# New costs in the emission clock of a two-layer diffusion block: TensorE, ScalarE and the port that VectorE shares with GpSimd

## The chip, the cores and the metric

The kernel runs on one core of a Trainium2 chip. A core has five engines with an instruction queue each: TensorE (matmuls, in the profile PE, with its weight loads as PEld), VectorE (DVE), ScalarE (ACT), GpSimd (POOL) and SyncE (SP, which here only issues transfers). Each works through its own queue in the order in which the program put instructions there, and they wait for one another by semaphores. The metric is the device time of one execution in microseconds (us); lower is better.

## The reference

Two layers work on 512 latent tokens and 256 context tokens of width 1024, in float32. A layer is

```
h += 0.5*gate * swiglu(modulate(rmsnorm(h)), w_gu, w_down)   # FFN 1, hidden width 2816
h += gate * (concat(retention, fourier, attention, gmlp)(modulate(rmsnorm(h)) @ w_in) @ w_out)
h += 0.5*gate * swiglu(modulate(rmsnorm(h)), w_gu, w_down)   # FFN 2
```

Shift, scale and gate come from `silu(cond) @ ada_w + ada_b`, nine vectors of 1024 for each layer, one set for the latent tokens and one for the context. Retention runs in both directions with a decay per head, the Fourier part is a two-dimensional transform, attention has four query and two key heads with normalized and rotated keys, and gMLP gates by a mix over chunks of 128 tokens. The context is not carried past the mixing of the last layer. At the end stands an RMS norm of the latent tokens.

## The kernel before, in words

**Arithmetic.** The activations stand transposed in SBUF (tile `H`: features on partitions, 768 tokens along the free side). Every weight block of 128x512 is read from HBM into a `raw` tile and split into a high and a low part (`w`): ScalarE casts the high part to fp32r, and VectorE or GpSimd subtracts it from the block to give the low part. The moving side is split in the same way, and a product is three matmuls (`mm3`: high·high, high·low, low·high; L241 and L243). Most FFN blocks are multiplied by Strassen's scheme in Winograd's form, seven products where eight would stand, whose sums and differences of blocks are made on GpSimd (weights, `w_sums`, written back into `raw`) and on VectorE or GpSimd (activations, `t_task` and `hid_sums`).

**Order.** Nothing is scheduled by a compiler: the program is written out by Python generators ("tasks") that are run by a small event loop (`run`, L179). Each task yields a time, or a condition, at which it wants to go on. The loop has one clock, `k.t`, which is the modelled end of the last matmul put out, and picks the task of the highest priority whose time is not later than `k.t`. If there is none, the clock is moved on. So the modelled cost of an instruction decides nothing on the chip by itself; it decides which instruction is put next into each engine's queue, and for some operations into whose queue.

The model is small. Each matmul adds to the clock in `pe` (L228). Each of VectorE (`V`), ScalarE (`A`) and GpSimd (`G`) has a clock of its own, moved in `Eng.__call__` (L126) by a fixed cost, plus the free size over a rate, plus a cost for each operand of one element. `Times` keeps, for each 64 columns of each tile, when it is written and read, and a hop of 110 ns between engines.

**Where the modelled clocks decide.** Four places matter here.

- `w_copies` (L429) puts out the next weight cast when `A.t <= k.t + slack`, `w_subs` (L441) the next weight subtraction when `V.t <= k.t + slack`, with a slack of 1500 ns for the two blocks that TensorE needs next, of 600 for the two after them and of 200 beyond; or at once where TensorE's task already asks for the block (`force`). A block that lies three or more ahead goes to GpSimd if `G.t <= k.t < V.t`.
- `any2` (L218) gives a subtraction, sum or product of two SBUF operands to the engine that would end it first: `max(V.t, k.t) + 68 + n/0.96` against `max(G.t, k.t) + 100 + n/0.42`.
- `norm_task` (L963) gives the addition of the shift to VectorE or to ScalarE by a comparison of the same kind (L995), and goes on to the next feature block when `V.t <= k.t + 1000`.
- Everything else yields the modelled time at which its operand is ready (`at`, `rdy`).

In an FFN stage the work on TensorE is one task (`ffn`: `pair`, seven products of 24 matmuls for each pair of hidden blocks; `down_fast` and `down`, the second matrix), so its order is given, and only the batches of the modulation product (`ada`, eight matmuls of 256 columns by `mmq`, L254) are put between. In a mixing stage some ten tasks share TensorE. `hid_task` (L1103) makes SiLU times the second half and splits it, `hid_sums` (L1272) the sums for `down_fast` (L1317), `t_task` (L1065) those for `pair`. `upd` (L1425) adds a finished PSUM bank to `H` on VectorE.

Of the kernel before, what the change touches and what calls it, by code (L numbers as in the profile page):

```python
# [39 lines left out]
def _free(ap):  # L40
    n = 1
    for x in ap.shape[1:]:
        n *= x
    return n
# [8 lines left out]
class Times:  # L53


    def __init__(self):
        self.tiles = {}
        self.rings = {}
        self.live = set()
        self.last = {}  # L60
        self.seq = 0
# [57 lines left out]
class Eng:  # L119
# [6 lines left out]
    def __call__(self, name, *args, cost=None, **kw):  # L126
        getattr(self.eng, name)(*args, **kw)  # L127
        aps = [x for x in list(args) + list(kw.values()) if hasattr(x, "tensor")]
        out = aps[0]
        n = max(_free(x) for x in aps)  # L130
        if cost is None:
            cost = self.fixed + n / self.rate + self.ptr * sum(1 for x in aps if _free(x) == 1)
        if name == "activation" and args[2] in TABLES and args[2] != self.table:
            self.table = args[2]
            cost += 1283.0
        writes = [out] + ([kw["accum_out"]] if "accum_out" in kw else [])
        self.t = self.k.T.op(self.num, self.t, cost, aps[1:], writes)
        return self.t + HOP


class Kernel:
    FAR, SB, NS = 3, 130.0, 3
    RP = 2
    NM, NK = 3, 0
    HV, SL = 4, 1500.0
# [4 lines left out]
    def __init__(self, tc, I, out, pools):  # L150
        self.tc, self.nc, self.I, self.out = tc, tc.nc, I, out
        self.pools = pools
        self.t = 0.0
        self.tick, self.cols, self.cold = 0, 0.0, True
        self.T = Times()
        self.V = Eng(self, tc.nc.vector, 1, 68.0, 0.96, 60.0)
        self.A = Eng(self, tc.nc.scalar, 2, 88.0, 1.2, 93.0)
        self.G = Eng(self, tc.nc.gpsimd, 3, 100.0, 0.42, 0.0)
        self.dt = 0.0
        self.tasks = []  # L160
        self.flags = set()
        self.mcols = [16, 0]
        self.mod0 = self.rawlim = 0
        self.ulive = 0
        self.nready = {}
        self.ps = pools["ps"].tile([P, 4096], F32, tag="b", name="b", bufs=1)
        self.psn = self.T.psn = self.ps.tensor.name
        self.free = set(range(8))
        self.T.add(self.ps, 4096, 0.0)
        self.nacc = {}  # L170
        self.nrs = {}
        self.hcnt = {}
# [55 lines left out]
    def pe(self, cols, rows, floor, reads, out):  # L228

        start = self.T.op(0, self.t, 0.0, reads, [out])  # L230
        k = int(start // TICK)
        if k != self.tick:
            self.cold = k > self.tick + 1 or self.cols < 3060.0
            self.tick, self.cols = k, 0.0
        cost = max(cols / 1.2 if self.cold else 2.5 + cols / 2.4, floor)
        self.cols += cols * rows / 128.0
        self.t = self.T.op(0, start, cost, reads, [out])

# [11 lines left out]
    def mmq(self, out, k, x, start, stop):  # L250


        q = 32 * (k % 4)
        self.nc.tensor.matmul(out[q:q + 32], self.cs[:, k], x, start=start, stop=stop)  # L254
        self.pe(2 * _free(x), 128, 60.0, [self.cs[:, k], x], out)

    def mm3(self, out, a, b, start, stop, more=False):
        self.mm(out, a[0], b[0], start, False, more)
# [1302 lines left out]
    def ret_core(self, l, p):  # L1561
# [27 lines left out]
        for i in range(2):  # L1589
# [4 lines left out]
            for q0, nq, keys in parts:  # L1594
                po = None
                pend = []
                for ki in range(len(keys) + 2):
                    if ki < len(keys):
# [11 lines left out]
                        yield  # L1610
                    if len(pend) > self.RP or ki >= len(keys) and pend:
                        kj, kt, t, ok = pend.pop(0)
# [639 lines left out]
```

## Time and profile before

| | |
|---|---|
| time, median of 3 runs | 2707.93 us (2704.53 to 2708.25) |
| profiled execution: its time | 2709.11 us |
| profiled execution: its span, first to last instruction | 2707.0 us |
| busy TensorE / VectorE / GpSimd / ScalarE | 96% / 74% / 50% / 47% |
| mean granted TensorE clock | 0.99 |
| matmul records | 17308 |

The span is 2.1 us less than the execution's own time. An engine's busy share is an average over stages; for TensorE the ends of matmuls are modelled by the profile, so 96% doesn't mean that it works at its peak in all that time. A time in ns behind a count in a row is the mean of one instruction; where an instruction waits for a port in the middle of its work, that wait is in its time.

### The profile page before, as it was taken

The numbers are of one execution on the slowest core, as the hardware profiler recorded it, in microseconds if no ns is written. First come the engines' busy times: TensorE is split into PE (matmuls) and PEld (weight loads), VectorE is DVE, ScalarE is ACT, GpSimd is POOL, SyncE is SP. The second block draws the span as 40 slices with busy tenths as digits, with TensorE's granted clock in tenths as the row PEclk, the third lists the DMA queues.
The fourth block names the chain that finished last, engine by engine and source line by source line (L and its number), as shares of the span: only waits on it lengthen the run. The fifth ranks groups of instructions, "written<-read, shape, count | busy, mean of one in ns | idle before, by whom it ended". The sixth has DMA issues, their size and how long they took to land.

```text
span 2707.0 us, 45375 instructions
## 1 busy us (share of the span) xinstructions
PE 2611.7 (96%) x17308; PEld 2442.5 (90%) x17308; DVE 2014.0 (74%) x3473; ACT 1269.3 (47%) x2620; POOL 1345.2 (50%) x1094
## 2 busy tenths in 40 slices
PE   7999999999999999999999989999999999999998
PEld 5888999998797988888999989999999797999998
DVE  5765787877578785656887877878878677877776
ACT  5433444455645554343444534444446545544445
POOL 3535666733222253546765547668734231654443
PEclk9999999999999999999999999999999999999999
DMA  8456222121111145553123111221232111122332
GB/s 289 138 167 210 71 70 87 63 81 55 51 44 47 40 144 191 172 187 109 63 63 102 55 47 63 64 93 63 63 104 63 51 60 42 48 94 94 105 99 78
DMA packets 242778, 252.62 MB, mean 93 GB/s; under 512 B 12188, under 2 KB 226432, under 8 KB 242560
## 3 DMA queue, kind: packets, MB, share of 16 engines
q1 hardware_dynamic: 236304, 246.82, 28.5%
q10 hardware_dynamic: 6256, 2.90, 0.4%
q8 instruction: 136, 2.23, 0.3%
q14 instruction: 82, 0.67, 0.1%
HBM read 247.59 MB, written 2.10 MB: 92 GB/s over the span
## 4 chain that ended last, share of the span: by engine, by line
PE 72%; DVE 18%; issue 3%; ACT 2%; DMA 2%; POOL 2%; SPq 0%; ACTq 0%; DVEq 0%; POOLq 0%
PE b L241 41%; PE b L243 28%; DVE u L127 7%; DVE w L127 6%; DVE t L127 3%; PE b L254 2%; PE b L282 2%; DVE H L127 2%; DMA raw<-in_ffn_w_gu_dram 1%; ACT w L127 1%; DMA u<-in_ada_w_dram 1%; ACT u L127 1%; ACT t L127 1%; POOL u L127 0%; POOL raw L127 0%
## 5 line engine op out<-in xcount | busy, mean ns | idle before, releaser
L241 PE MATMUL b<-u,w 128*128 128x384 f32 (+1 forms) x8736 | 1465.3, 326 | 30.7 <-DVE u L127 21.4
L241 PEld LDWEIGHTS b<-u,w 128*128 128x128 f32 x8736 | 1424.0, 189 | 61.0 <-DVE u L127 28.9
L127 ACT CAST w<-raw 128x512 fp32r<-128x512 f32 x949 | 578.9, 621 | 626.9 <-PE b L241 255.2
L127 DVE TENSOR_TENSOR w<-raw,w 128x512 fp32r<-128x512 f32 x688 | 663.0, 972 | 231.4 <-ACT w L127 219.6
L127 POOL TENSOR_TENSOR raw<-raw 128x512 f32<-128x512 f32 x416 | 616.9, 1504 | 397.2 <-DMA raw<-in_ffn_w_gu_dram 138.1
L127 POOL TENSOR_TENSOR w<-raw,w 128x512 fp32r<-128x512 f32 x261 | 371.0, 1433 | 543.6 <-ACT w L127 495.2
L243 PE MATMUL b<-u,w 128*128 128x256 f32 (+2 forms) x3888 | 590.9, 309 | 17.7 <-ACT u L127 5.8
L243 PEld LDWEIGHTS b<-u,w 128*128 128x128 f32 x3888 | 543.0, 194 | 44.8 <-issue 10.2
L127 DVE SCALAR_TENSOR_TENSOR H<-b,modG,H 128x128 f32<-128x128 f32 (+3 forms) x832 | 368.5, 474 | 154.1 <-PE b L243 85.4
L243 PE MATMUL b<-w,u 128*128 128x256 f32 x2172 | 286.6, 288 | 1.8 <-DVE w L127 1.8
L243 PEld LDWEIGHTS b<-w,u 128*128 128x128 f32 x2172 | 270.0, 192 | 12.0 <-issue 6.8
L127 ACT COPY t<-b 128x384 f32<-128x384 f32 (+5 forms) x287 | 123.5, 431 | 209.6 <-PE b L241 98.1
L127 ACT CAST u<-u 128x384 fp32r<-128x384 f32 (+4 forms) x318 | 140.8, 464 | 121.1 <-DVE u L127 103.1
L127 DVE TENSOR_TENSOR u<-u 128x384 fp32r<-128x384 f32 (+8 forms) x227 | 183.0, 819 | 12.9 <-ACT u L127 12.1
L127 POOL TENSOR_TENSOR u<-u 128x384 fp32r<-128x384 f32 (+2 forms) x137 | 123.0, 907 | 93.2 <-ACT u L127 92.5
L243 PE MATMUL b<-u 128*64 128x256 f32 (+7 forms) x516 | 141.1, 371 | 0.0
L127 DVE TENSOR_TENSOR t<-t,b 128x384 f32<-128x384 f32 (+3 forms) x216 | 106.2, 494 | 43.3 <-PE b L241 42.3
L127 POOL TENSOR_TENSOR nacc<-nacc,t 128x256 f32<-128x256 f32 (+2 forms) x112 | 89.7, 802 | 95.6 <-ACT t L127 91.6
L127 ACT CAST u<-t 128x384 fp32r<-128x384 f32 (+2 forms) x162 | 74.1, 471 | 114.1 <-DVE t L127 107.3
L243 PEld LDWEIGHTS b<-u 128*128 128x128 f32 (+2 forms) x516 | 81.6, 176 | 47.0 <-issue 34.4
L127 ACT CAST u<-b 64x256 fp32r<-64x256 f32 (+3 forms) x175 | 77.9, 454 | 75.3 <-PE b L282 72.7
L127 POOL TENSOR_TENSOR rs<-mse,mhalf 128x2 f32<-128x2 f32 (+4 forms) x41 | 45.1, 1104 | 115.4 <-DVE mse L127 106.1
(95 smaller groups left out, 1660.7 us busy)
## 6 DMA issues: line engine op xcount, KB each, us to landing
raw<-in_ffn_w_gu_dram SPq DMA_DIRECT2D x176, 512.0 KB
adaraw<-in_ada_w_dram SPq DMA_DIRECT2D x113, 512.0 KB
raw<-in_ffn_w_down_dram SPq DMA_DIRECT2D x88, 512.0 KB
raw<-in_w_in_dram SPq DMA_DIRECT2D x28, 512.0 KB
raw<-in_w_out_dram SPq DMA_DIRECT2D x32, 256.0 KB
u<-in_ada_w_dram SPq DMA_DIRECT2D x15, 512.0 KB
u<-in_ada_w_dram SPq DMA_DIRECT2D x16, 384.0 KB
raw<-in_w_in_dram SPq DMA_DIRECT2D x16, 256.0 KB
```

The costliest lines, as they stand in the source:

```text
L127: getattr(self.eng, name)(*args, **kw)
L241: self.nc.tensor.matmul(out, a, b, start=start, stop=stop, skip_group_check=True)
L243: self.nc.tensor.matmul(out, a, b, start=start, stop=stop)
L254: self.nc.tensor.matmul(out[q:q + 32], self.cs[:, k], x, start=start, stop=stop)
L282: self.nc.tensor.transpose(out, in_, self.ident[:p, :p])
```

## The change

Four costs of the emission's clock are changed. No instruction, tile, buffer or transfer of the kernel is added or removed by hand; what may change is the order in each queue, and which of two engines gets an operation.

```diff
         writes = [out] + ([kw["accum_out"]] if "accum_out" in kw else [])
+        ins = aps[1:]
+        if self.num == 1 and sum(1 for x in ins if _free(x) > 8) > 1 and all(x.tensor.name != self.k.psn for x in ins):
+
+            start = max(self.t, self.k.t)
+            cost += self.k.SHARE * max(0.0, min(self.k.G.t, start + cost) - start)
         self.t = self.k.T.op(self.num, self.t, cost, aps[1:], writes)
...
+    PF, SHARE = 13.3, 0.5
...
-        self.A = Eng(self, tc.nc.scalar, 2, 88.0, 1.2, 93.0)
+        self.A = Eng(self, tc.nc.scalar, 2, 150.0, 1.25, 50.0)
...
-        cost = max(cols / 1.2 if self.cold else 2.5 + cols / 2.4, floor)
+        cost = max(cols / 1.2 if self.cold else self.PF + cols / 2.4, floor)
...
-        self.pe(2 * _free(x), 128, 60.0, [self.cs[:, k], x], out)
+        self.pe(_free(x), 128, 60.0, [self.cs[:, k], x], out)
```

The first part: a VectorE instruction (`num` 1) with two or more inputs of over 8 elements, none of them in PSUM, costs half as much again for the part of it during which GpSimd's modelled clock says GpSimd is at work. The second: ScalarE's fixed cost, rate and cost of a one-element operand. The third: a matmul of n columns at the full clock costs 13.3 + n/2.4 ns where it cost 2.5 + n/2.4. The fourth: a matmul of the modulation product counts its columns once where it counted them twice.

## Rows read from the trace of the kernel before

**Rows 1.** The page: busy time, share of the span, instructions of three engines.

```profile
PE 2611.7 (96%) x17308; PEld 2442.5 (90%) x17308; DVE 2014.0 (74%) x3473; ACT 1269.3 (47%) x2620; POOL 1345.2 (50%) x1094
```

**Rows 2.** Waits of TensorE, whole span: who waited for whom, us, times, longest.

```profile
PE b L241 <- DVE u L127: 21.4, 21, 2.0
PE b L243 <- ACT t L127: 12.2, 9, 3.8
PE b L282 <- DVE t L127: 8.9, 7, 1.8
...
PE b L243 <- DVE w L127: 2.3, 3, 1.2
```

**Rows 3.** Chain that ended last, 300 to 400 us: start, length, what.

```profile
301.06 1.70 DVE w L127
...
306.29 74.47 PE b L241 x428
...
386.98 1.70 DVE w L127
388.68 2.04 DVE t L127 x2
390.72 1.70 DVE w L127
392.42 0.53 DVE H L127
392.95 0.47 DVE u L127
393.42 0.04 issue
393.46 1.34 PE b L241 x6
```

**Rows 4.** Windows: PE, PEld, DVE, ACT, POOL busy (instructions), granted clock, DMA share, GB/s.

```profile
375.00:400.00 25.00, 23.27 (x133) 22.63 (x132) 21.54 (x25) 11.61 (x24) 20.79 (x15) 1.00 0.08 24
1550.00:1575.00 25.00, 22.20 (x127) 21.56 (x125) 24.89 (x32) 13.37 (x26) 14.52 (x11) 1.00 0.14 43
1575.00:1600.00 25.00, 20.45 (x99) 20.05 (x100) 18.96 (x37) 4.70 (x9) 6.42 (x5) 0.80 0.00 1
2350.00:2375.00 25.00, 19.77 (x149) 19.34 (x149) 20.00 (x38) 10.18 (x22) 22.23 (x16) 0.86 0.07 22
```

**Rows 5.** Timeline, 104 to 112 us: a modulation batch between FFN products.

```profile
106.70 1.07 PE L254 MATMUL b<-adaraw,cs 128*32 128x256 f32 x16
107.70 1.31 PE L241 MATMUL b<-u,w 128*128 128x384 f32 x6
```

**Rows 6.** Groups of instructions by form: busy us, mean ns, idle before.

```profile
L127 DVE TENSOR_TENSOR w<-raw,w 128x512 fp32r<-128x512 f32 x688 | 663.0, 972 | 231.4 <-ACT w L127 219.6 <-PE b L254 2.1
L127 ACT CAST w<-raw 128x512 fp32r<-128x512 f32 x949 | 578.9, 621 | 626.9 <-PE b L241 255.2 <-PE b L243 138.5 <-POOL raw L127 100.6
L127 DVE SCALAR_TENSOR_TENSOR H<-b,modG,H 128x256 f32<-128x256 f32 x432 | 204.1, 475 | 69.5 <-PE b L243 68.4
L127 DVE TENSOR_SCALAR u<-u,M 128x256 f32<-128x256 f32 x60 | 29.4, 490 | 0.2
L127 ACT ACTIVATE u<-u,M 128x256 f32<-128x256 f32 x44 | 22.3, 506 | 33.2 <-DVE u L127 33.2
```

**Rows 7.** Tile `w`: duration ns min/median/max of VectorE's and GpSimd's subtractions.

```profile
L127 DVE TENSOR_TENSOR w<-raw,w x688: 674/693/1792, 21.0 to 2671.6; 128x512 fp32r<-128x512 f32 x172
L127 POOL TENSOR_TENSOR w<-raw,w x261: 1265/1301/2117, 38.8 to 2670.1; 128x512 fp32r<-128x512 f32 x131
```

**Rows 8.** Timeline, 1551 to 1562 us, VectorE and GpSimd at the same time.

```profile
1556.58 1.33 POOL L127 TENSOR_TENSOR t<-u 128x384 f32<-128x384 f32 x1
1556.95 1.37 DVE L127 TENSOR_TENSOR u<-u 128x384 f32<-128x384 f32 x1
...
1558.24 0.55 DVE L127 TENSOR_TENSOR u<-t,u 128x384 fp32r<-128x384 f32 x1
```

**Rows 9.** Timeline of TensorE, 1570 to 1600 us, with its idle time before.

```profile
1574.14 0.62 PE L243 MATMUL b<-u,w 128*128 128x384 f32 x2 [2.55 <-DVE u L127]
1577.83 0.69 PE L243 MATMUL b<-u,w 128*128 128x384 f32 x1 [3.07 <-ACT u L127]
1580.23 14.87 PE L243 MATMUL b<-u,w 128*128 128x384 f32 x68 [1.72 <-DVE u L127]
```

## The prediction

> **What bounds the kernel now.** I read the page first. TensorE is busy for 2611.7 us of 2707.0 [rows 1], so all its idle time together is 2707.0 − 2611.7 = 95.3 us. The change puts out the same instructions, so only this idle time and the granted clock can move; the rest is a floor. The reader should then see in TensorE's waits [rows 2] that no releaser holds much of it: the largest is VectorE's `u` before L241, 21.4 us in 21 places, about 1.0 us each; then come some 9 to 12 us each that belong to the mixing stages (L243 on ScalarE's `t`, L282 on VectorE's `t`). Weights proper (`DVE w`) cost it 2.3 us in 3 places.
>
> The chain of waits tells what lies behind those 1.0 us [rows 3]. At 393.46 us TensorE starts again after a wait; followed back, VectorE ran without a gap through two weight subtractions of 1.70 us, two sums of `hid_sums` (2.04), an update of `H` (0.53) and the sum `u` (0.47) which TensorE wanted. Another such subtraction stands at 301.06 before the stop at 303.80. So where an FFN pair hands over to `down_fast`, work for later weights stands in VectorE's queue ahead of work that TensorE waits for. The window shows the same: 23.27 us of PE in 25, with VectorE at 21.54 and GpSimd at 20.79 [rows 4].
>
> The second place is the start of a stage. From 1550 to 1575 us VectorE is busy for 24.89 of 25 us; from 1575 to 1600 TensorE does 20.45 us of work, at a mean granted clock of 0.80 (1.0 is 2.4 GHz), and from 2350 to 2375 it does 19.77 at 0.86 [rows 4].
>
> **What the new costs say, against the trace.** TensorE: the chain has 428 matmuls of 384 columns in 74.47 us, 174.0 ns each [rows 3]. The old cost is 2.5 + 384/2.4 = 162.5 ns, the new one 13.3 + 160 = 173.3. So the old clock gains 11 ns on TensorE at each matmul. The Trainium skill (TensorE: Matmul & The Clock Gate, Back-to-back issue gap) gives N/2.4 + 2.5 ns for the warm gap of an isolated matmul; for 384 columns that is the old cost, 11.5 ns under the row, and by it the new clock would be 7% too slow and the weights would be put out too early. The row decides for the new one.
>
> A modulation batch: eight calls (16 records) start at 106.70 and the next matmul at 107.70, 125 ns a call [rows 5]; old 2.5 + 512/2.4 = 216, new 13.3 + 256/2.4 = 120. ScalarE: a weight cast takes 621 ns [rows 6]; old 88 + 512/1.2 = 515, new 150 + 512/1.25 = 560. VectorE: a weight subtraction takes 693 ns in the middle, 972 in the mean and 1792 at most [rows 6, 7]; old 68 + 512/0.96 = 601, new 601 to 901, by what GpSimd is modelled to do. The excess is GpSimd's: at 1556.95 a VectorE sum runs 1.37 us beside a GpSimd operation, the next one, alone, 0.55 [rows 8]. What stays short is VectorE's work on PSUM: an update of `H` by 256 columns takes 475 ns [rows 6], and the model keeps 68 + 267 + 60 = 395.
>
> **Part by part, as time.** All terms stand against the profiled execution (2709.11 us, of which 2.11 lie outside its span); that is 1.18 over the median of 2707.93.
>
> 1. *Weight subtractions in front of the sums.* With GpSimd busy a subtraction moves VectorE's clock by up to 300 ns more, so the gate `V.t <= k.t + slack` (1500, 600 or 200 ns) shuts earlier. Against this each matmul moves `k.t` by 10.8 ns more, 0.26 us in 24 matmuls, which opens it again. So the gate is tighter only where GpSimd is modelled busy, which is in just these bursts (20.79 of 25 us, [rows 4]), and easier elsewhere. One subtraction fewer in front of the wanted sum is worth 0.69 us (alone) to 1.78 us, which is more than half of the 1.0 us that a place costs. I take it that this comes about in half of the 21 places: −21.4/2 = −10.7 us. Bounds: 0 (the blocks are among the next two, or asked for, so the gate doesn't hold them) and −21.4. A subtraction put off is late next for the matmul that uses it: 3 more waits like today's, 2.3 us in 3 places [rows 2], cost at most +2.3; I take +1.
>
> 2. *Starts of stages.* `norm_task` sends the addition of a shift to ScalarE when VectorE's clock leads by over 171 ns (181 + 256/1.2 − 90 − 256/1.92). VectorE's lead grows with the new port cost, ScalarE's only by some 45 ns an operation. An addition costs VectorE 490 ns and ScalarE 506 [rows 6], and ScalarE has room: 13.37 of 25 us [rows 4]. Six additions moved at the starts save VectorE 6 x 0.49 = 2.9 us; I take −3. Bounds: 0, and −8, the loss of the window 1575 to 1600 (99 matmuls) against a full one at the pace of [rows 3], 25/0.174 = 144 matmuls: 45 x 0.174 = 7.8 us. The three waits there last 2.55, 3.07 and 1.72 us [rows 9]; the rest is the clock at 0.80.
>
> 3. *More goes to GpSimd.* `any2` compares a VectorE clock that is now later with an unchanged GpSimd clock (a sum of 384 columns: 468 against 1014 ns), and a weight block three ahead goes there if `V.t > k.t`. Nothing in the change makes GpSimd dearer. In a burst this doesn't pay: a 384-column sum moved takes 0.55 us off VectorE and makes the one that runs beside it 1.37 instead of 0.55 [rows 8], +0.27 us net; a moved subtraction −0.69 + (1.78 − 0.69) = +0.40. The bursts are 12 (four fast groups in each of three of the four FFN stages). One sum more in each: 12 x 0.27 = +3.2; I take +3.5. Bounds: 0, and three subtractions in each, 36 x 0.40 = +14.
>
> 4. *Mixing.* There TensorE's clock becomes right while VectorE's PSUM work stays 80 ns an instruction too cheap, so a matmul behind it may be put out a little early; ScalarE's dearer copies work the other way. The waits it touches are those on `t`, 12.2 + 8.9 us [rows 2]. I take 0, with −5 and +6 as bounds (a quarter of 21.1 either way, rounded).
>
> 5. *Modulation batches.* In a stretch of 30 matmuls and one batch the old clock was 30 x 11.5 = 0.35 us short and 8 x 91 = 0.73 us long, so 0.38 us slow in all; the new one is within 0.1 us. TensorE works without a gap there (the FFN's matmuls go on 1.00 us after the batch's start [rows 5]), and the batches only fill. 0, hidden by the FFN's own matmuls; −2 to +2 if it isn't.
>
> 6. *ScalarE's costs.* 949 casts each 45 ns later in a model of an engine that is 47% busy [rows 1, 6]: 0, its effects are in terms 2 and 4.
>
> Sum: −10.7 + 1 − 3 + 3.5 = −9.2 us, so 2709.11 − 9.2 = 2699.9 for the profiled execution, and 1.2 less as a median: **2699 us** (−0.33%).
>
> **The rivals.**
>
> *No change.* In the FFN stages TensorE has a single task, and the order in each chain (last product, SiLU, product, split, sums) is given by data. Where the next two weight blocks are concerned the gate hardly holds anything. For it speaks that 74.47 us pass without one stop and that TensorE is at 96%; against it, that weight work is on the chain right before the stops [rows 3]. Terms 1 to 4 near their zero bounds, about 2706 us.
>
> *Slower by GpSimd.* Term 3 near its upper bound with term 1 at half: VectorE's lateness pushes sums and subtractions to GpSimd, whose operations then hold VectorE's, which makes both late in the bursts. −5 + 14 + 1 = +10 us, and with term 4's +2 about 2720 us. It decides from the point where two or more operations go over in each burst: 24 x 0.40 = 9.6 eats term 1. For it speaks VectorE's 1792 ns against 693 [rows 7]; against it, that GpSimd is itself at 20.79 of 25 us in a burst [rows 4], so that its clock seldom is free. The Trainium skill (SBUF — State Buffer, Who interferes with whom) says that the shared port is an exclusive lock which holds the other engine for a whole instruction; by that even a cost of half the overlap is too low, and the trace agrees that far as 0.55 becomes 1.37 beside a 1.33 us operation.
>
> *Much faster.* Terms 1, 2 and 4 near their lower bounds: −18 − 6 − 3 + 3 = −24, about 2684 us, if the starts of stages lose their stops and with them the low clock.
>
> **How the numbers follow.** Some 0.2%, 5.4 us, is about what a measurement of this kernel can tell from no change. My forecast (2688 to 2702) has 0.38, much faster 0.08, no change 0.22, slower 0.32 (of which about a quarter above 2722). So faster 0.46, same 0.22, slower 0.32. The range takes in both signs: 2684 to 2722 leaves out some 0.06 below and 0.09 above. The forecast's own range is 2688 to 2702.
>
> **What would show it.** Right: TensorE's wait for VectorE's `u` before L241 falls from 21.4 to about 11 us; the count of weight subtractions on VectorE stays near 688; fewer of them stand on the chain in front of a stop. Term 2: more than 44 additions of 256 columns on ScalarE, and a PE busy time above 20.45 and 19.77 us in the windows that answer to [rows 4]. Term 3: GpSimd's 261 subtractions, and the mean of VectorE's 972 ns, tell how much went over. What would make it wrong: over 290 subtractions on GpSimd with a mean of VectorE's above 1050 ns (the second rival), new waits of TensorE on `DVE w` above 5 us (work put off too far), or longer stops in mixing, where one reordered softmax or retention task can cost more than all the bursts give.

## The result and the profile after

The changed kernel takes 2740.72 us in the median (2737.69 to 2742.58, 4 runs) against 2706.23 for the kernel before beside it: a ratio of 1.0127, 95% interval 1.0109 to 1.0144. It is 34 us slower where 9 us less were forecast, and outside the range.

The first reading is the page, busy time by engine, beside [rows 1], and with it the span and the mean granted TensorE clock.

```profile
PE 2626.4 (96%) x17308; PEld 2451.7 (89%) x17308; DVE 2036.1 (74%) x3447; ACT 1272.9 (46%) x2619; POOL 1369.1 (50%) x1121
...
core 0: 2740.8 us, clock 0.985
```

The span grew by 33.8 us. TensorE's busy time grew by 2626.4 − 2611.7 = 14.7 us with the same 17308 matmul records, and its idle time from 95.3 to 2740.8 − 2626.4 = 114.4, by 19.1. The busy part is the clock: the missing share of the granted clock was 0.010 of 2707.0 us, 27 us, and is now 0.015 of 2740.8, 41 us; the difference of 14 us is about what TensorE worked longer. Where the 14 us lie is seen in two stretches, before and after (columns as in [rows 4]):

```profile
40.00:140.00 100.00, 91.47 (x620) 76.91 (x618) 70.02 (x122) 49.12 (x112) 51.97 (x43) 0.97 0.54 176
860.00:900.00 40.00, 40.00 (x238) 31.39 (x237) 32.16 (x58) 21.37 (x43) 3.84 (x3) 1.00 0.09 27
...
40.00:140.00 100.00, 90.06 (x575) 74.81 (x574) 68.41 (x117) 46.54 (x107) 48.58 (x41) 0.91 0.52 163
860.00:900.00 40.00, 40.00 (x186) 30.25 (x185) 28.56 (x49) 19.38 (x36) 5.08 (x4) 0.83 0.09 27
```

The first lost 3 us of the full clock and now loses 9, the second none and now 6.8. In the second TensorE is busy for all of the 40 us in both kernels. So a part of the work at the low level (1.2 GHz) follows stops, as after the one of 4.30 us below, but another part stands where TensorE did not stop.

TensorE's waits answer to [rows 2]: engine, line and tile, releaser, us in total, times, longest. L247, L249 and L288 of the changed kernel are L241, L243 and L282 of before.

```profile
PE b L249 <- ACT t L127: 15.1, 12, 4.3
PE b L249 <- ACT u L127: 14.7, 5, 7.8
PE b L247 <- DVE u L127: 13.0, 11, 2.3
PE b L288 <- DVE t L127: 9.7, 7, 2.7
PE b L247 <- ACT w L127: 8.7, 8, 1.2
PE b L249 <- DVE w L127: 6.1, 7, 2.3
...
PE b L247 <- ACT t L127: 3.8, 5, 0.9
```

Here the reader sees where the forecast was right and what it missed. The wait for VectorE's `u` before the FFN's seven-product matmuls (L241, now L247) did fall, from 21.4 to 13.0 us. But ScalarE has become the larger releaser, and the idle time before these matmuls, whoever ended it, did not fall: 30.7 us before, 32.9 after (lines of the two pages).

```profile
L241 PE MATMUL b<-u,w 128*128 128x384 f32 (+1 forms) x8736 | 1465.3, 326 | 30.7 <-DVE u L127 21.4
...
L247 PE MATMUL b<-u,w 128*128 128x384 f32 (+1 forms) x8736 | 1469.1, 327 | 32.9 <-DVE u L127 13.0
```

Over all its tiles TensorE waits for ScalarE for 45.1 us in 34 places where it was 20.3 in 15, while VectorE as a direct releaser went from 49.0 to 43.9.

The subtractions of tile `w` (minimum, median and maximum in ns), beside [rows 7], and by form, beside [rows 6]:

```profile
L127 DVE TENSOR_TENSOR w<-raw,w x662: 674/693/1808, 21.0 to 2705.0; 128x512 fp32r<-128x512 f32 x166
L127 POOL TENSOR_TENSOR w<-raw,w x287: 1261/1317/2024, 37.8 to 2699.1; 128x512 fp32r<-128x512 f32 x144
...
L127 DVE TENSOR_TENSOR w<-raw,w 128x512 fp32r<-128x512 f32 x662 | 625.6, 953 | 243.8 <-ACT w L127 229.7 <-PE b L260 4.4 <-PE b L247 0.5
...
L127 ACT ACTIVATE u<-u,M 128x256 f32<-128x256 f32 x45 | 22.8, 507 | 35.1 <-DVE u L127 35.1
```

Only 26 subtractions went over to GpSimd (261 to 287), and VectorE's mean is not longer (972 to 953 ns). One addition of a shift moved to ScalarE (44 to 45).

The windows that answer to [rows 4], at the same stage starts (columns as there):

```profile
1575.00:1600.00 25.00, 16.73 (x94) 16.01 (x92) 24.10 (x32) 10.85 (x21) 15.89 (x12) 0.87 0.14 42
2375.00:2400.00 25.00, 17.56 (x124) 16.57 (x124) 24.84 (x42) 8.84 (x18) 19.40 (x14) 0.80 0.13 41
```

Either has less TensorE work than any of before in [rows 4], 16.73 and 17.56 us. But the starts lie later here, so single windows don't compare well. Over a whole start, 1500 to 1650 and 2300 to 2450 us, before and after:

```profile
1500.00:1650.00 150.00, 141.07 (x870) 139.03 (x870) 117.72 (x212) 69.69 (x154) 78.12 (x75) 0.97 0.16 51
2300.00:2450.00 150.00, 141.38 (x1141) 139.78 (x1140) 118.13 (x205) 74.41 (x166) 80.83 (x70) 0.97 0.24 78
...
1500.00:1650.00 150.00, 138.93 (x877) 137.03 (x876) 117.19 (x217) 68.85 (x153) 69.47 (x70) 0.97 0.19 59
2300.00:2450.00 150.00, 138.29 (x1076) 131.92 (x1075) 123.63 (x213) 78.44 (x171) 72.12 (x63) 0.97 0.22 68
```

TensorE's idle time grew by some 2 and 3 us, and the clock is 0.97 in all four: the starts are slower, but no longer at the low level.

How ScalarE comes to hold TensorE is seen in the timeline from 93 to 103 us (start, length, engine, operation, number, in brackets the engine's idle time before it and its releaser):

```profile
92.53 5.92 POOL L127 TENSOR_TENSOR raw<-raw 128x512 f32<-128x512 f32 x3
93.31 5.96 DVE L127 TENSOR_TENSOR u<-u 128x768 fp32r<-128x768 f32 x3
...
100.46 0.54 DVE L127 TENSOR_TENSOR t<-t,b 128x384 f32<-128x384 f32 x1
101.03 0.51 ACT L127 CAST u<-t 128x384 fp32r<-128x384 f32 x1 [5.20 <-DVE t L127]
101.45 0.61 ACT L127 CAST w<-raw 128x512 fp32r<-128x512 f32 x1
101.97 0.36 ACT L127 COPY t<-b 128x256 f32<-128x256 f32 x1
...
102.39 1.02 PE L249 MATMUL b<-sel,t 128*128 128x2 f32 x4 [4.30 <-ACT t L127]
```

TensorE, idle since 98.09 us, waits for the copy that runs at 101.97; the copy's input has been ready since the modulation batch ended at about 96.8 us. The copy stands in ScalarE's queue behind a cast (101.03) that waits for a sum of VectorE, and VectorE is held up: three subtractions of 768 columns, whose pace in the model is 68 + 768/0.96 = 868 ns, take 5.96 us, 2 us each, beside GpSimd's work (92.53). Four of the same form take 3.57 us, 0.9 each, where GpSimd stands idle during nearly all of it (its next instruction starts at 1591.38, after 3.39 us of idle time):

```profile
1588.62 3.57 DVE L127 TENSOR_TENSOR u<-u 128x768 fp32r<-128x768 f32 x4 [0.18 <-ACT u L127]
```

ScalarE sits idle for 5.20 us with the wanted copy behind it, and TensorE for 4.30. The next 24 matmuls of 384 columns take 6.93 us, 0.29 each, where 30 take 5.45 us some 9 us later (112.64): the mean granted clock from 100 to 120 us is 0.83. The kernel before has a stop of this form too, so the mechanism is not new, only more frequent:

```profile
84.86 1.01 PE L243 MATMUL b<-sel,t 128*128 128x2 f32 x4 [3.76 <-ACT t L127]
```

The other large stop, 7.8 us on `ACT u`, is at the start of the second layer. The chain of waits from 1590 to 1601 us (start, length, what), and TensorE's own line:

```profile
1592.11 0.31 DVE w L127
...
1593.79 1.23 DVE modG L127
...
1595.53 1.75 DVE w L127
1597.28 0.53 DVE H L127
1597.80 0.46 DVE t L127
...
1598.86 0.69 PE L249 MATMUL b<-u,w 128*128 128x384 f32 x1 [7.82 <-ACT u L127]
```

TensorE is stopped from 1591.0 to 1598.9. The sum `t` that it needs (through a cast) runs at 1597.80; before it in VectorE's queue stand weight subtractions, the small `modG` and an update of `H`. In [rows 9] the same start had three waits, 2.55 + 3.07 + 1.72 = 7.3 us, so one long stop has taken the place of three.

### The profile page after: what moved, and what is told of

Read it like the earlier page. It is cut to its first block, busy times and chain, and to the rows that moved or that the text cites. A ratio compares the mean times of both kernels' runs of the same rounds, so it can differ in the third digit from the quotient of the medians.

```text
span 2740.8 us, 45426 instructions
## 1 busy us (share of the span) xinstructions
PE 2626.4 (96%) x17308; PEld 2451.7 (89%) x17308; DVE 2036.1 (74%) x3447; ACT 1272.9 (46%) x2619; POOL 1369.1 (50%) x1121
## 4 chain that ended last, share of the span: by engine, by line
PE 65%; DVE 20%; issue 5%; ACT 4%; POOL 3%; DMA 2%; SPq 0%; ACTq 0%; DVEq 0%; POOLq 0%
PE b L247 38%; PE b L249 24%; DVE u L127 8%; DVE w L127 5%; DVE t L127 4%; PE b L260 2%; ACT u L127 2%; DVE H L127 2%; PE b L288 2%; ACT w L127 2%; DMA raw<-in_ffn_w_gu_dram 1%; POOL nacc L127 1%; POOL raw L127 1%; POOL rs L127 1%; ACT t L127 1%
## 5 line engine op out<-in xcount | busy, mean ns | idle before, releaser
L247 PE MATMUL b<-u,w 128*128 128x384 f32 (+1 forms) x8736 | 1469.1, 327 | 32.9 <-DVE u L127 13.0
L247 PEld LDWEIGHTS b<-u,w 128*128 128x128 f32 x8736 | 1427.7, 189 | 63.7 <-issue 17.9
L127 DVE TENSOR_TENSOR w<-raw,w 128x512 fp32r<-128x512 f32 x662 | 625.6, 953 | 243.8 <-ACT w L127 229.7
L127 POOL TENSOR_TENSOR w<-raw,w 128x512 fp32r<-128x512 f32 x287 | 408.2, 1433 | 564.0 <-ACT w L127 551.3
L249 PE MATMUL b<-u,w 128*128 128x256 f32 (+2 forms) x3888 | 588.3, 308 | 21.4 <-ACT u L127 14.7
L249 PEld LDWEIGHTS b<-u,w 128*128 128x128 f32 x3888 | 540.2, 193 | 48.8 <-ACT u L127 16.6
L249 PE MATMUL b<-w,u 128*128 128x256 f32 x2172 | 287.1, 288 | 4.9 <-DVE w L127 4.9
L249 PEld LDWEIGHTS b<-w,u 128*128 128x128 f32 x2172 | 271.1, 193 | 13.6 <-DVE w L127 5.7
L127 ACT COPY t<-b 128x256 f32<-128x256 f32 (+5 forms) x287 | 123.1, 431 | 191.6 <-PE b L247 93.2
L127 POOL TENSOR_TENSOR u<-u 128x384 fp32r<-128x384 f32 (+2 forms) x150 | 132.4, 889 | 102.0 <-ACT u L127 98.7
L249 PE MATMUL b<-u 128*128 128x256 f32 (+7 forms) x516 | 145.0, 381 | 2.8 <-DVE u L127 2.8
L127 DVE TENSOR_TENSOR u<-t,u 128x384 fp32r<-128x384 f32 (+3 forms) x153 | 127.5, 844 | 16.8 <-ACT u L127 16.6
L249 PEld LDWEIGHTS b<-u 128*128 128x128 f32 (+2 forms) x516 | 84.6, 183 | 52.9 <-issue 37.4
```

What stands on the lines that cost most here:

```text
L247: self.nc.tensor.matmul(out, a, b, start=start, stop=stop, skip_group_check=True)
L249: self.nc.tensor.matmul(out, a, b, start=start, stop=stop)
```

## The experiments

Every time is a median; the ratio, and the us with a sign, are against runs of the kernel before on the same chip. Four theories were set against each other: **PORT** (VectorE's port cost drives work to GpSimd), **PE** (TensorE's new cost makes the loss, for which RATIO, MARGIN and GATE below are reasons), **TUNED** (any step off the old costs loses), and the forecast's own view that the new costs help.

**The four costs one at a time.** Each is the kernel before with one part of the diff.

```diff
-        cost = max(cols / 1.2 if self.cold else 2.5 + cols / 2.4, floor)
+        cost = max(cols / 1.2 if self.cold else 13.3 + cols / 2.4, floor)
```

> Of the four costs only TensorE's is changed (13.3 + n/2.4 ns). Theory PORT (VectorE's new port cost pushes subtractions and sums to GpSimd, and that makes the loss): this kernel has no port cost, so it is within 5 us of before (about 2707 us) and GpSimd keeps about 261 weight subtractions. Theory PE (TensorE's slower clock is what opens the weight gates earlier and takes away the margin by which dependent matmuls were put out late): most of the loss is here, 2725 to 2740 us. Theory TUNED (the old costs stand at a point found for the whole set of slacks, and leaving it by any cost loses some 10 to 30 us, without a special culprit): 2715 to 2735 us.

Measured: 2761.86 us, +53, ratio 1.0196 (1.0181 to 1.0211). It is slower than the whole change and above every range given.

```diff
+        if self.num == 1 and sum(1 for x in ins if _free(x) > 8) > 1 and all(x.tensor.name != self.k.psn for x in ins):
+            start = max(self.t, self.k.t)
+            cost += 0.5 * max(0.0, min(self.k.G.t, start + cost) - start)
```

> Only VectorE's port cost is added (half the overlap with GpSimd's clock). Theory PORT: nearly all of the loss, 2730 to 2745 us, with some 285 weight subtractions on GpSimd. Theory PE: within 5 us of before or a little faster, 2695 to 2712 us, since VectorE's clock comes nearer to its measured times. Theory TUNED: 2715 to 2735 us.

Measured: 2730.96 us, +22, ratio 1.0084 (1.0069 to 1.0099), with 298 subtractions on GpSimd. Its FFN waits:

```profile
PE b L246 <- DVE u L127: 17.6, 17, 2.1
PE b L246 <- ACT u L127: 14.4, 6, 2.6
```

In all TensorE waits 45.5 us for ScalarE here, as much as after the whole change.

```diff
-        self.A = Eng(self, tc.nc.scalar, 2, 88.0, 1.2, 93.0)
+        self.A = Eng(self, tc.nc.scalar, 2, 150.0, 1.25, 50.0)
```

> Only ScalarE's costs are changed (a 128x512 cast 560 ns where it was 515). Theories PORT and PE: within 5 us of before, about 2707 us, as ScalarE is busy for 47% only. Theory TUNED: a loss here too, 2712 to 2735 us, although the new costs are nearer to the 621 ns of the trace.

Measured: 2709.74 us, +1, ratio 1.0009 (0.9998 to 1.0021).

```diff
-        self.pe(2 * _free(x), 128, 60.0, [self.cs[:, k], x], out)
+        self.pe(_free(x), 128, 60.0, [self.cs[:, k], x], out)
```

> Only the columns of the modulation matmuls are counted once. Theories PORT and PE: within 5 us of before, with any change in the two stretches that hold the batches (50 to 300 and 1000 to 1280 us). Theory TUNED: a loss of 5 to 20 us.

Measured: 2705.60 us, −3, ratio 0.9990 (0.9980 to 0.9999).

So PE is right that the largest loss is here, TUNED in its plain form falls (two of four steps cost nothing), and PORT holds for a part only. The four add up to 53 + 22 + 1 − 3 = 73 us where the whole change loses 34, so they do not add. The changed kernel with TensorE's old cost was not run. The kernel with TensorE's cost alone shows, in its waits:

```profile
PE b L243 <- ACT u L127: 17.8, 4, 7.9
PE b L243 <- ACT t L127: 15.7, 12, 4.5
PE b L241 <- DVE u L127: 12.9, 15, 2.0
PE b L241 <- ACT w L127: 11.1, 10, 1.2
PE b L282 <- DVE t L127: 11.0, 8, 2.6
PE b L282 <- DVE nacc L127: 10.4, 7, 2.6
PE b L241 <- ACT t L127: 9.0, 5, 2.0
```

The same picture as after the whole change, and stronger: a shorter wait for VectorE's `u` in the FFN, but more waits there in all (39.7 us where it was 30.5), and 56.0 us of waits for ScalarE. Of the 49.3 us by which its span is longer, 32 are idle time of TensorE and 17 are busy time.

**Why TensorE's cost.** The first two of these are the kernel before with another fixed cost of a matmul, the other two the run with 13.3 ns with one thing more.

```diff
-        cost = max(cols / 1.2 if self.cold else 2.5 + cols / 2.4, floor)
+        cost = max(cols / 1.2 if self.cold else 3.0 + cols / 2.4, floor)
```

> Before, with 3.0 ns for a matmul's fixed cost where it was 2.5: half a nanosecond, which means nothing on the chip but changes the order in every queue. A measure of how far a reordering alone moves the time. Theory TUNED (any step off the old costs loses): 2720 to 2740 us, as other costs did. Theories RATIO and MARGIN (below), by which the size of the step counts: within 8 us of before.

Measured: 2714.93 us, +6, ratio 1.0024 (1.0014 to 1.0033). In this one sample a reordering that means nothing moves the kernel by some 6 us; differences of that size and smaller are not read below.

```diff
-        cost = max(cols / 1.2 if self.cold else 2.5 + cols / 2.4, floor)
+        cost = max(cols / 1.2 if self.cold else -6.0 + cols / 2.4, floor)
```

> Before, with TensorE's clock moved the other way: n/2.4 - 6 ns, 154 ns for 384 columns where 173 are measured. Theory MARGIN (a clock that is too quick puts a dependent matmul out later than the operand is ready, and that time covers what the model leaves out): no loss, 2695 to 2712 us. Theory RATIO (the clocks of VectorE and ScalarE were short by about as much as TensorE's, so that their ratio was right before): a loss of 10 to 30 us, on the other side. Theory TUNED: 2720 to 2745 us.

Measured: 2732.79 us, +24, ratio 1.0091 (1.0076 to 1.0106). MARGIN expected no loss: on this side it misses, and RATIO and TUNED both had this time in their ranges.

```diff
             cost += 1283.0
+        cost *= 1.08
...
-        v = max(self.V.t, self.t) + self.V.fixed + n / self.V.rate
-        g = max(self.G.t, self.t) + self.G.fixed + n / self.G.rate
+        v = max(self.V.t, self.t) + 1.08 * (self.V.fixed + n / self.V.rate)
+        g = max(self.G.t, self.t) + 1.08 * (self.G.fixed + n / self.G.rate)
```

> TensorE's new cost as in the run with it alone, and every modelled cost of VectorE, ScalarE and GpSimd times 1.08, so that their ratio to TensorE's clock is about that of before; the hop, the slacks of the gates and the other waits in ns stay. Theory RATIO: back to 2700 to 2720 us from 2762. Theory MARGIN: half way at most, 2730 to 2755 us, since the hop is not larger. Theory TUNED: 2735 to 2765 us.

Measured: 2745.28 us, +37, ratio 1.0138 (1.0121 to 1.0156). The ratio of the engines' clocks gives back 17 of 53 us, not all: RATIO misses, as far as this run tests it, since the hop, the slacks and the transfers kept their ns. MARGIN and TUNED had this time in their ranges.

```diff
-HOP = 110.0
+HOP = 200.0
```

> TensorE's new cost as in the run with it alone, and a hop between engines of 200 ns where it was 110, which gives each handover a margin again and leaves the engines' costs. Theory MARGIN: back to 2705 to 2725 us from 2762, with TensorE's waits on ScalarE's and VectorE's tiles in the mixing stages near those of before. Theory RATIO: 2745 to 2770 us. Theory TUNED: 2735 to 2765 us.

Measured: 2732.08 us, +23, ratio 1.0081 (1.0064 to 1.0098). The larger hop gives back 30 of 53 us, the most of the three, though less than MARGIN had in its bounds; the waits for ScalarE fell only from 56.0 to 48.7.

**The same questions on the whole change.** Each of these four is the changed kernel with one edit.

```diff
-HOP = 110.0
+HOP = 200.0
```

> The changed kernel with a hop of 200 ns between engines in the clock, where it was 110. Theory MARGIN (instructions of ScalarE and VectorE are put out as soon as the modelled operand is ready, the real one comes later, and what stands behind in the same queue is held up until TensorE waits): 2712 to 2725 us, as the larger hop took 30 us off the run with TensorE's cost alone, and TensorE's waits on ScalarE fall from 45 to about 30 us. Theory GATE (weight casts and subtractions are let in too early, since TensorE's clock moves on more per matmul): within 8 us of 2741.

Measured: 2725.85 us, +19, ratio 1.0062 (1.0040 to 1.0084): at MARGIN's upper bound, with 36.4 us of waits for ScalarE where about 30 were expected.

```diff
-    SN, SWA, SWV, SS, SE, SC, ST = 1000.0, 4000.0, 1500.0, 1000.0, 600.0, 100.0, 500.0
+    SN, SWA, SWV, SS, SE, SC, ST = 1000.0, 4000.0, 1500.0, 1000.0, 600.0, -150.0, 500.0
```

> The changed kernel, with tasks that feed ScalarE, VectorE or GpSimd resumed 150 ns after the modelled operand is ready, where they were resumed 100 ns before it (250 ns later in all; matmuls keep their time). Theory MARGIN: 2715 to 2730 us, and ScalarE's own waits for VectorE's u and t (295 us in the changed kernel) fall below 260. Theory GATE: within 8 us of 2741. A loss is possible under both if chains become longer by 250 ns a link: 2745 to 2765 us.

Measured: 2723.88 us, +17, ratio 1.0056 (1.0034 to 1.0077). The time fell as MARGIN said, and TensorE's waits for ScalarE from 45.1 to 29.9 us; but ScalarE's own waits for VectorE's `u` and `t` hardly did (290 us), which that theory had below 260. ScalarE waits as long; what stands behind it is less often what TensorE wants.

```diff
-    SN, SWA, SWV, SS, SE, SC, ST = 1000.0, 4000.0, 1500.0, 1000.0, 600.0, 100.0, 500.0
+    SN, SWA, SWV, SS, SE, SC, ST = 1000.0, 2000.0, 700.0, 1000.0, 600.0, 100.0, 500.0
```

> The changed kernel with tighter gates for weight work: a slack of 700 ns for subtractions where it was 1500, and of 2000 for casts where it was 4000. Theory GATE: 2712 to 2728 us. Theory MARGIN: within 10 us of 2741, or slower by waits of TensorE on weights (6 us in the changed kernel, then above 10).

Measured: 2745.36 us, +39, ratio 1.0137 (1.0117 to 1.0157). GATE falls, as far as slacks of half the size can tell: weight work let in too early isn't the cause. (Casts have a slack of their own: 4000 ns for the next two blocks, where the part on the kernel gives the subtractions' 1500 for both.)

```diff
-    PF, SHARE = 13.3, 0.5
+    PF, SHARE = 13.3, 0.0
```

> The changed kernel without VectorE's port cost (TensorE, ScalarE and modulation costs alone). Theory PORT (the port cost adds a loss of its own, as the run with it alone lost 22 us): 2715 to 2735 us, faster than the changed kernel. Theory RATIO or MARGIN: the port cost makes VectorE's clock later and so takes back a part of what TensorE's new cost loses, so without it 2752 to 2770 us.

Measured: 2748.31 us, +42, ratio 1.0143 (1.0116 to 1.0169). Beside TensorE's new cost the port cost doesn't lose 22 us; with it the time is some 7 us lower, hardly more than a reordering alone moved. PORT falls as the cause of the whole; RATIO and MARGIN, from 2752 us on, were a little too high. ScalarE's and the modulation's costs, free alone, go with 12 us less beside TensorE's (+42 where it alone has +53). One wait of this run bears on term 1:

```profile
PE b L247 <- DVE u L127: 6.8, 12, 0.9
```

**Is it the new clock, and how much of it?** The first two are the kernel before with the larger hop or the later resumption of the diffs above (110 to 200; 100 to −150), the third the changed kernel with both.

> The kernel before, with the tasks that feed ScalarE, VectorE or GpSimd resumed 150 ns after the modelled operand is ready (before: 100 ns ahead of it). Theory MARGIN (the old, too quick clock of TensorE held that margin already): no gain, 2705 to 2725 us. Theory FREE (a later resumption helps under any clock and has nothing to do with the new costs): 2685 to 2698 us.

Measured: 2721.93 us, +15, ratio 1.0051 (1.0034 to 1.0068). The edit that gave 17 us to the changed kernel takes 15 from the one before.

> The kernel before with a hop of 200 ns where it was 110. Theory MARGIN: no gain, 2705 to 2730 us. Theory FREE: 2685 to 2698 us.

Measured: 2698.12 us, −9, ratio 0.9968 (0.9958 to 0.9979). MARGIN (2705 us or more) misses, and the time is at FREE's upper bound. This edit helps under the old clock too, so not all of its gain under the new one is an answer to the new costs. TensorE's waits in this run:

```profile
PE b L243 <- ACT u L127: 13.5, 6, 7.6
...
PE b L241 <- POOL u L127: 9.1, 8, 1.9
PE b L241 <- ACT w L127: 7.9, 7, 1.3
...
PE b L241 <- DVE u L127: 4.1, 8, 1.2
```

The FFN's wait for VectorE's `u` is 4.1 us where it was 21.4, and all waits for ScalarE and VectorE together 60.3 us where they were 69.3 before and 89.0 after the change. Waits for ScalarE alone don't tell the time: here they are 36.1 us and the kernel is the faster one.

> The changed kernel with both margins, the hop of 200 ns and the later resumption. Theory MARGIN, with the whole loss in it: 2700 to 2715 us. If only half of the loss is of that kind and the rest is that slacks and limits fit the old clock (theory TUNED for the rest): 2718 to 2732 us, no better than with either.

Measured: 2716.71 us, +10, ratio 1.0033 (1.0021 to 1.0045): between the two bounds given.

```diff
-        return max(self.T.ready(x) for x in aps)
+        return max(self.T.ready(x) for x in aps) + 150.0
...
-    SN, SWA, SWV, SS, SE, SC, ST = 1000.0, 4000.0, 1500.0, 1000.0, 600.0, 100.0, 500.0
+    SN, SWA, SWV, SS, SE, SC, ST = 1000.0, 4000.0, 1500.0, 1000.0, 600.0, 250.0, 500.0
```

> The changed kernel where only what waits for readiness by the full time, matmuls and transposes, is resumed 150 ns later; what feeds ScalarE, VectorE and GpSimd keeps its time, 100 ns ahead of readiness. If the margin acts on TensorE's queue (a matmul put out too early stops all that stands behind it): 2718 to 2730 us. If it acts on the queues of ScalarE and VectorE, as the later resumption of their tasks suggests: within 8 us of 2741.

Measured: 2735.62 us, +28, ratio 1.0100 (1.0085 to 1.0115). Putting out the matmuls later gives 6 us, no more than a reordering alone moved; putting out what feeds the other engines later gave 17. (Five places in the program that don't go through `at` resume 150 ns earlier in this run, so it isn't quite pure.)

**The rest.** The changed kernel with both margins, the hop at 290 ns; and the kernel before with the modulation cost and a hop of 200 ns.

> The changed kernel with the later resumption (150 ns after readiness) and a hop of 290 ns. Theory MARGIN for the whole loss: 2695 to 2710 us. If the rest is of another kind: 2713 to 2735 us, as chains also become longer with each larger hop.

Measured: 2707.83 us, ratio to before 1.0004 (0.9994 to 1.0014): the whole loss is gone. The kernel before with these two margins at their full size was not run, so it isn't shown that they answer to the new costs alone. Of its waits, the two that answer to the largest above:

```profile
PE b L249 <- ACT u L127: 18.2, 7, 7.0
PE b L247 <- DVE u L127: 18.0, 23, 1.2
```

The long stop at a stage's start is still there (7.0 us); all waits for ScalarE are 34.3 us where they were 45.1.

> The kernel before with the new modulation cost and a hop of 200 ns, the two edits that lost nothing alone (2706 and 2698 us). If such gains add: 2693 to 2699 us, faster than both kernels. If a small reordering moves the time by some 5 us either way: 2693 to 2710 us.

Measured: 2698.05 us, −8, ratio 0.9967 (0.9953 to 0.9980). The two gains don't add; it is level with the larger hop alone, and both are faster than the two kernels of this study.

## Why the prediction was wrong

**The step that failed** is the place of TensorE's new cost in the sum. The prediction saw that the old clock was 11 ns short at each matmul and took that only as 0.26 us in 24 matmuls that opens a gate (term 1), and as 0 with −5 and +6 in the mixing stages (term 4). Alone it measures +53 us, and with ScalarE's and the modulation's costs beside it, which are free alone, +42. The gate isn't how it works, as far as halved slacks tell (+39 against +34). How it works is argued from here on, not shown. The runs point to this: the clock is not a forecast of times by itself, it sets the distance between an instruction that makes an operand and the one that uses it, in matmuls. With 162.5 ns for a matmul of 173.3, a modelled delay of 1 us was 1.07 us of the chip; with 173.3 it is 1.00. What the model leaves out (2 us for a 768-column subtraction beside GpSimd where it has 0.87) may have been covered in part by that. Two results fit this. Margin given back by hand takes the loss away in steps: +34, then +17 to +19 with either, +10 with both, +2 with both and a hop of 290. And the later resumption changes sign with the clock: −17 us under the new, +15 under the old. Two results limit it. A still quicker clock (−6 ns) loses 24 us, so the old value stood near a best point of the whole set of constants and is not explained by margin alone. The rival that any far step from an order once tuned loses some 15 to 25 us (−6 ns, the port cost alone and the later resumption alone all do) stays open for a part of the 53. And the larger hop gains 9 us under the old clock too, so a part of its 15 us under the new is no answer to the new cost. Which single handovers carry the 53 us was not separated; TensorE's waits for ScalarE (20 to 56 us) are where most of its idle part shows. The port cost alone shows the same waits, so they are no mark of TensorE's cost.

**Term 1** met the size of one wait by luck: 13.0 us against the 11 forecast. The term gave that to the port cost, which shuts the gate. But without the port cost the wait is 6.8 us, with TensorE's cost alone 12.9, and with the port cost alone 17.6, beside a new wait for ScalarE of 14.4. So the port cost isn't what shortened it, and alone it loses 22 us where the terms that it carries (1 to 3) had −9.2. Its other side was mis-sized: work put off was given +1, and the waits for weights grew from 2.3 to 6.1 us on VectorE's half and by a new 8.7 us on ScalarE's, where in the stop looked at (1.15 us, at 416.92) a weight cast stands behind casts of activations that wait for VectorE.

**Term 2** failed: one addition moved, not six, and the stage starts became some 2 and 3 us slower, at the same mean clock of 0.97.

**Term 3**, and the second rival with it, had the right sign of the whole for a wrong reason. GpSimd got 26 subtractions more and VectorE's mean fell by 19 ns; the signs that were named for it (over 290 and over 1050 ns) didn't come. The port cost alone loses 22 us, with 298 subtractions on GpSimd and a mean of 1008 ns on VectorE, so only one of the two signs came there; whether this mechanism makes the 22 us is not shown; beside TensorE's new cost it goes with 7 less (+34 with it, +42 without), perhaps since it makes VectorE's clock later.

**Term 4** had a wrong premise besides its size: the model isn't 80 ns too cheap for VectorE's work on PSUM (last section). The waits that it named went from 21.1 to 24.8 us, within its bounds; the wait for ScalarE's `u` (5.8 to 14.7 us) was in no term.

**Terms 5 and 6** were right: −3 and +1 us where 0 was given.

**The low clock** was named only as a bonus of fewer stops at the starts of stages. It worked the other way, in other stretches, and is about 14 of the 33.8 us.

**The range** was built from bounds of the terms, each of one place. None held a case in which a common time base moves every handover of the kernel at once.

## What to carry to other kernels

In an emission by a modelled clock, an error that all handovers share can be part of the tuning: here a truer cost of one engine lost 53 us alone, and with the hop and the resumption times moved as well nothing was lost. So such a cost should be tried together with them, not costed by the gates that read the clock. When several costs change at once, run each alone first; here two were free, one lost more than the whole, and one that lost 22 us alone lost nothing in company. And when a forecast wait comes true, look whether it does so without the part that was to cause it. Look for the releaser behind the releaser: TensorE waited for ScalarE, ScalarE's queue stood for VectorE, and VectorE for the port.

## What the runs showed of the hardware that had not been expected

The mean duration of an instruction is not the time that it takes from its engine. In the kernel before, ScalarE runs three weight casts back to back (timeline of ScalarE, 1565 to 1575 us):

```profile
1569.74 1.66 ACT L127 CAST w<-raw 128x512 fp32r<-128x512 f32 x3
```

Three in 1.66 us at 0.62 us each [rows 6] are (1.66 − 0.62)/2 = 0.52 us apart. The old cost of 515 ns was ScalarE's pace; the new 560 ns, which the prediction set beside the 621 ns of the row, is not. VectorE shows the same in [rows 3]: a sum of 384 columns takes 0.47 us on the chain, as the old 468 ns have it, and 0.55 us as one instruction [rows 8]. And so do its updates of `H`, here two of 384 columns (timeline of VectorE, 386 to 398 us):

```profile
392.34 0.60 DVE L127 SCALAR_TENSOR_TENSOR H<-b,modG,H 128x384 f32<-128x384 f32 x1
393.33 1.13 DVE L127 SCALAR_TENSOR_TENSOR H<-b,modG,H 128x384 f32<-128x384 f32 x2
```

They are 1.13 − 0.60 = 0.53 us apart, and the model has 68 + 400 + 60 = 528 ns; the prediction compared the model with the longer time of one instruction. TensorE's 173.3 ns is a pace, taken from a run of matmuls, so of TensorE's and ScalarE's new costs only TensorE's was measured in the sense that the clock uses.

A change that leaves TensorE's 17308 matmuls as they are moved its busy time by 14.7 us, nearly as much as its idle time (19.1), and the granted clock accounts for about all of it. Nearly half of this lies in a stretch (860 to 900 us) in which TensorE has no gap.
